# Adding transfers of a recurrence stage issued from one spaced list that is held during norms, with more descriptor space and later taps

## The chip, the cores and the metric

The kernel runs on one core of one Trainium2 chip. The metric is the device time of one launch in microseconds (us), the median of several executions. The core has five engines that run their own instruction streams: TensorE (PE) for matrix products, VectorE (DVE) and ScalarE (ACT) for elementwise work, GpSimd (POOL), and SyncE (SP), which here does nothing but issue transfers. Transfers move between the device memory (DRAM) and the on-chip memory by 16 DMA engines. They are issued on two queues: SP's, and POOL's own, which the profile calls software dynamic and whose descriptors are written into a small space on the chip; its size is an argument of the program (`dynamic_dma_scratch_size`). [...]

## The reference, cut to what matters

A decoder trunk of two layers on a sequence of 1024 vectors of 1024 numbers, all in float32. Layer 0 mixes by a gated recurrence with 8 heads, layer 1 by a causal convolution of width 31; behind each stands a layer norm, a squared-ReLU network of width 4096, and another layer norm.

```python
for i in range(DEPTH):
    mix = hgrn2_mixer(...) if i % 2 == 0 else conformer_conv_mixer(...)
    x = layer_norm(DEEPNORM_ALPHA * x + mix, ...)
    ff = jnp.square(jax.nn.relu(x @ ffn_w1[i])) @ ffn_w2[i]
    x = layer_norm(DEEPNORM_ALPHA * x + ff, ...)

def hgrn2_mixer(h, w_in, lb, norm_g, w_out):
    q, fz, v, g = jnp.split(h @ w_in, 4, axis=-1)
    f = lb + (1 - lb) * sigmoid(fz); k = 1 - f; q = silu(q)
    o = recurrence(q, k, v, cumsum(log f))      # S_t = diag(f_t) S_{t-1} + k_t v_t,  o_t = S_t q_t
    o = o * lax.rsqrt(jnp.mean(jnp.square(o), axis=-1, keepdims=True) + RMS_EPS)   # the norm of a head
    return (o * norm_g * silu(g)) @ w_out
```

## The kernel before, in words

Each float32 product is made of three products of a cheaper kind (high by high, high by low, low by high part). Larger products are moreover done on 2 by 2 blocks with 7 products for 8; their operands are sums of blocks, the "forms", which are numbered 1 to 7 and run in the order `ORDER` (1, 2, 6, 5, 7, 3, 4).

For the second matrix of each network (`ffn_w2`, 16 blocks of 4 parts in all, each part 0.5 MB) these sums of blocks are made in DRAM by transfers alone, with no engine's arithmetic. One such **chain** is written by `block_sums` (L401): two copies of 1 MB (L419 and L420), an accumulate of 1 MB onto what the first copy wrote (L421), and two accumulates of 0.5 MB, each onto the next slice (L423, twice). Each accumulate needs what the one before it wrote, so POOL, which issues all of them, waits for the landing of the last before it issues the next. Twelve chains are issued during the recurrence stage, one at every sixth form; the others come later, beside the network, and there `block_sums` is called with `after` or `adds`.

The **recurrence stage** takes the span from about 60 to 440 us. It interleaves two things. One is twelve pairs of half-width products (`PAIRS`: eight for q and forget gate, four for the output gate), 7 forms each, with weight blocks loaded as `pr` (L585), forms made from them as `fs`, and results copied out by `evacuate` (t at L837). The other is the recurrence of the eight heads, each a Python generator (`recurrence(h)`) that issues one small step whenever `slot()` calls `step()`. Time in the program is counted in **ticks**, one for each slot of three matrix products. `later(n, job)` has a job issued n ticks on. All engines are under a manual schedule here, so this order of writing is the order in which each engine runs; nothing is reordered afterwards. Outside this stage a scheduler sets the order.

At its end a head yields its two **norms**, one for each half of the sequence. `settle(half)` lets ScalarE square the outputs (L735), POOL scale the sum and raise it to the power -1/2 (L736, and L518 in `power_m_half`), and, 4 ticks later, ScalarE scale the outputs (L741); `give(half)` then lets TensorE transpose them (`ident,o`). The norms of a head come as a pair, a few us apart; there are 16. Outputs go to DRAM (`od`), come back (`u`, L962 and others), are multiplied by the gate, and stored again (`zd`, L924).

The **seam** (`seam()`) is the last stretch of the stage: within the last gate pair the output matrix `wout` is loaded (L940), the gated heads come back (L950), and the last head fetches its values at L632 (`f<-vd`, two loads of 256 KB) only just ahead of use, into a buffer that has just become free.

In the convolution stage (about 1125 to 1500 us) the 31 taps of each channel are scalars in a small table `par`, loaded at the start; ScalarE (L1591), VectorE (L1603) and POOL share the convolution. Products run beside it, in the order of `SEQ`, with weights that are either read from DRAM ready made (`wa<-ready`, L81) or loaded raw (L90) and split by ScalarE and VectorE (L72). There are three raw buffers, and a load into one first waits on POOL by a copy of one column (L86).

Of the kernel before, what the change touches and what calls it, by code (L numbers as in the profile page):

```python
# [8 lines left out]
F32 = mybir.dt.float32  # L9
# [3 lines left out]
ALU = mybir.AluOpType  # L13
PSUM = bass.MemoryType.PSUM

P = 128
# [15 lines left out]
QSCALE = 2.0**-30  # L32

NRM, LB, BPW1, BDW, CLG, CLB, TAP = 0, 8, 16, 32, 40, 48, 56
NPAR = TAP + KB * TAPS

KBYTES = 220
PAIRS = [("q", 0), ("q", 1), ("q", 2), ("q", 3), ("g", 0), ("q", 4), ("q", 5), ("q", 6), ("g", 1), ("q", 7), ("g", 2), ("g", 3)]
NPOOL = (12, 11)
SEQ = "P00 P01 P02 P03 P04 P05 P06 P07 P10 P11 P12 P13 N0 P14 F0 P15 S0 P16 P17 UA0 UA1 E2 E3 N1 E4 F1 E5 E6 S1 E7 UB0 UB1 L2 L3 L4 L5 L6 L7"  # L40
# [228 lines left out]
def body(ctx, tc, d, out):  # L269
# [100 lines left out]

    order = ExitStack()
    order.enter_context(tc.manual_schedule(engines={getattr(mybir.EngineType, e) for e in ("PE", "Pool", "SP", "DVE", "Activation")}))
    par = cst.tile([P, NPAR], F32, name="par")
    ident = cst.tile([P, P], F32, name="ident")
    wide_t, rows = (HT,), (NTB, P)

# [3 lines left out]
    vd = [[dram.tile([P, NTB, HT], F32, name=f"vd{m}{n}") for n in range(2)] for m in range(2)]  # L380

    ticks, waiting = [0], []

    def later(n, job):
        if n:
            waiting.append((ticks[0] + n, job))
        else:
            job()

    def tick(n=1):  # L390
        for _ in range(n):
            ticks[0] += 1
            for at, job in [w for w in waiting if w[0] <= ticks[0]]:
                waiting.remove((at, job))
                job()

    sums = {}

    def block_sums(name, layer, c, after=None, gap=0, adds=None):

        t = sums[name, layer, c] = dram.tile([4, P, 1024], F32, name=f"sum_{name}{layer}{c}")  # L401
        v, w = t.rearrange("a p n -> p a n"), d[name][layer, c].rearrange("a p n -> p a n")
        queue = nc.sync if after is not None else nc.gpsimd
        if adds is not None:

            def copies(rows, after):
                nc.sync.dma_start(out=t[0:4:2, rows.start, 0:1], in_=after)
                queue.dma_start(out=v[rows, 0:2], in_=w[rows, 0:4:2])
                queue.dma_start(out=v[rows, 2:4], in_=w[rows, 0:2])

            copies(slice(16, P), after)
            adds.append(lambda after: copies(slice(0, 16), after))
            adds.append(lambda after: nc.gpsimd.dma_start(out=v[:, 0:2], in_=w[:, 2:4], accum_op=ALU.add))
            for i in (2, 3):
                adds.append(lambda after, i=i: nc.gpsimd.dma_start(out=v[:, i], in_=v[:, i - 1], accum_op=ALU.add, max_dma_last_dim=4096))
            return
        if after is not None:
            nc.sync.dma_start(out=t[0:4:2, 0, 0:1], in_=after)
        queue.dma_start(out=v[:, 0:2], in_=w[:, 0:4:2])  # L419
        later(gap // 2, lambda: queue.dma_start(out=v[:, 2:4], in_=w[:, 0:2]))  # L420
        parts = [lambda: nc.gpsimd.dma_start(out=v[:, 0:2], in_=w[:, 2:4], accum_op=ALU.add)]  # L421
        for i in (2, 3):
            parts.append(lambda i=i: nc.gpsimd.dma_start(out=v[:, i], in_=v[:, i - 1], accum_op=ALU.add, max_dma_last_dim=4096))  # L423
# [83 lines left out]
    load_v(a2, 1, 0)  # L507
    load_v(a3, 1, 2)
    load_x(x11, 1, 4)
    nc.sync.dma_start(out=par, in_=d["par"])  # L510
    make_identity(nc, ident)
    nhalf = cst.tile([P, 8], F32, name="nhalf")
    nc.gpsimd.memset(nhalf, -0.5)
    qs = cst.tile([P, 1], F32, name="qs")
    nc.gpsimd.memset(qs, QSCALE)

    def power_m_half(dst, src, n):
# [116 lines left out]
    def recurrence(h):  # L634
# [96 lines left out]
        def settle(half):  # L731
            ss = stat.tile([P, 2, 4], F32, tag="ss", name="ss")
            cs = range(half * NTB, half * NTB + NTB)
            for c in cs:
                nc.scalar.activation(o[:, c], out_ps[:, c, :], AF.Square, scale=1.0 / QSCALE, accum_out=ss[:, 0, c % NTB : c % NTB + 1])  # L735
            nc.gpsimd.tensor_scalar(out=ss[:, 1], in0=ss[:, 0], scalar1=1.0 / P, scalar2=RMS_EPS, op0=ALU.mult, op1=ALU.add)  # L736
            power_m_half(ss[:, 0], ss[:, 1], 4)

            def rest():
                for c in cs:  # L740
                    nc.scalar.activation(o[:, c], out_ps[:, c, :], AF.Copy, scale=ss[:, 0, c % NTB : c % NTB + 1])  # L741
                later(1, lambda: ready.add(half))

            later(4, rest)
# [262 lines left out]
    for p, (kind, j) in enumerate(PAIRS):  # L1007
        st = {"banks": dict(turn_of)}
        turn_of = {"z": turn_of["a"], "a": turn_of["b"], "b": turn_of["z"]}
        pace[1] = 0.0 if p == 0 else 0.6 if p < 3 else 0.5  # L1010
        if kind == "g" and p < len(PAIRS) - 1:
            to_load += [(2 * j, 0), (2 * j + 1, 1), (2 * j, 1), (2 * j + 1, 0)]
        if p == len(PAIRS) - 1:
            seam()
        for i in ORDER:
            if kind == "q" and i == 2:
                while any(a[0] <= j - 3 for a in active) or recs and recs[0] <= j - 3:
                    tick()
# [15 lines left out]
    while step():  # L1034
        tick()
    tick(100)
    assert not waiting and not loaded and not to_load and not gates, (waiting, gates)
    order.close()
    oT = [o[0] for o in oT]

# [187 lines left out]
    class Up:  # L1228
# [14 lines left out]
        def settle(self, c):  # L1243

            for q in range(2):
                self.first(self.of[c], q)
# [291 lines left out]
    assert not ahead and not staged  # L1538


    nc.sync.dma_start(out=sm[:, :2], in_=d["lmix"])
    rings["mm"] = bank((1, 5, 2, 6))
    stA = {"hr": ring(run(0, 2, 8), (8, 256), "ha"), "r": ring(run(16, 2, 2), wide_t, "r")}
# [29 lines left out]
        bg.jobs.append(conv[-1])  # L1573

    def tap(j, i):
        return par[:, TAP + j * TAPS + i : TAP + j * TAPS + i + 1]

    def convolve_pool(half, j, u, sums):

# [380 lines left out]
```

## Time and profile before

| what | value |
| --- | --- |
| median of 3 runs | 2057.19 us (2056.47 to 2060.54) |
| profiled execution | 2057.16 us |
| its span, first to last instruction | 2055.4 us |
| recurrence stage, TensorE busy | 371.18 of 380.00 us (from 60 to 440) |
| convolution stage, TensorE busy | 373.08 of 375.00 us (from 1125 to 1500) |
| transfers on POOL's queue, whole span | 58.72 MB, 12.2% of the 16 DMA engines |

A row of the timeline gives the start in us, the time of the group in us, engine, line, operation, tiles (output<-inputs) and, in brackets, how long the engine had stood idle before and for what. "SPq" and "PEld" are SP's issues and TensorE's weight loads. In the view of waits, "issue" stands for time in which the engine waited for nothing that the profile shows. "DMA to landing" is the time from the issue of a transfer to the landing of its last byte.

### The profile page before, as it was taken

The page shows a single profiled execution, that of the slowest core. Times are in us where ns is not written, and L with a number is a line of the kernel's source. Part 1 is how long each engine was busy: PE and PEld are TensorE (multiplying, and loading weights), DVE is VectorE, ACT ScalarE, POOL GpSimd, SP SyncE. Part 2 cuts the span into 40 slices and gives each one's busy share as a digit, 9 for nine tenths or more (in the row PEclk, how much of TensorE's full clock was granted, in tenths as well). Part 3 has the DMA queues.
Part 4 walks back from the last instruction along what each step waited for, and adds up shares of the span by engine and source line. Part 5 has one row for each costly group of instructions (what it writes and reads, how often), then busy time and mean ns, then how long its engine had stood idle before and what let it go on. Part 6 is the DMA issues. An engine that isn't in the chain of part 4 may idle for free. (4 is left out here: it accounts for less than half of the span.)

```text
span 2055.4 us, 29649 instructions
## 1 busy us (share of the span) xinstructions
PE 2023.6 (98%) x11144; PEld 1669.0 (81%) x11144; DVE 1488.1 (72%) x1978; ACT 1094.5 (53%) x1725; POOL 396.3 (19%) x405
## 2 busy tenths in 40 slices
PE   8999999999999999999999999999999999999998
PEld 7888887888787888888888888888888878888886
DVE  8698888877856675665567897889589666754456
ACT  5456565631655556444443776498615555443343
POOL 0112232111101000000001798089110000100002
PEclk9999999999999999999999999999999999999999
DMA  4778999842679776989998744496759768995542
GB/s 187 221 201 229 265 254 269 248 183 85 192 268 295 281 282 225 394 329 329 338 335 299 298 185 184 180 351 247 276 216 337 231 225 303 391 292 195 195 154 103
DMA packets 183944, 517.55 MB, mean 252 GB/s; under 512 B 17912, under 2 KB 49784, under 8 KB 182776
## 3 DMA queue, kind: packets, MB, share of 16 engines
q1 hardware_dynamic: 168312, 456.93, 61.7%
q0 software_dynamic: 15488, 58.72, 12.2%
q8 instruction: 87, 1.43, 0.3%
q14 instruction: 57, 0.47, 0.1%
HBM read 380.85 MB, written 201.85 MB: 283 GB/s over the span
## 5 line engine op out<-in xcount | busy, mean ns | idle before, releaser
L204 PE MATMUL ps<-dw,dh 128*128 128x512 f32 x2688 | 611.3, 389 | 0.5 <-DVE dh L204 0.5
L204 PEld LDWEIGHTS ps<-dw,dh 128*128 128x128 f32 x2688 | 504.3, 188 | 105.3 <-DVE dh L204 0.9
L204 PE MATMUL ps<-x1f,fw 128*128 128x512 f32 x1344 | 307.5, 390 | 5.2 <-ACT c L1266 2.3
L204 PEld LDWEIGHTS ps<-x1f,fw 128*128 128x128 f32 x1344 | 251.5, 188 | 59.7 <-issue 2.5
L204 PE MATMUL ps<-xf,fs 128*128 128x512 f32 x1008 | 248.6, 397 | 3.6 <-issue 1.7
L204 POOL TENSOR_TENSOR cb<-cb,prod 128x512 f32<-128x512 f32 x168 | 223.2, 1337 | 13.0 <-ACT prod L1591 2.4
L204 PEld LDWEIGHTS ps<-xf,fs 128*128 128x128 f32 x1008 | 184.0, 188 | 42.6 <-issue 1.9
L204 DVE TENSOR_TENSOR dh<-dh 128x1024 fp32r<-128x1024 f32 x112 | 136.5, 1222 | 109.4 <-ACT dh L72 109.3
L204 DVE SCALAR_TENSOR_TENSOR ps<-u,par,ps 128x512 f32<-128x512 f32 x296 | 206.0, 750 | 10.6 <-ACT ps L1603 9.3
L204 PE MATMUL ps<-xa,wa 128*128 128x512 f32 x864 | 203.3, 392 | 0.2
L72 ACT CAST dh<-dh 128x1024 fp32r<-128x1024 f32 x112 | 117.5, 1051 | 143.9 <-DMA dh<-hf 137.7
L72 ACT CAST dw<-dr 128x1024 fp32r<-128x1024 f32 x112 | 117.4, 1054 | 140.9 <-PE ps L204 125.5
L204 DVE TENSOR_TENSOR dw<-dr,dw 128x1024 fp32r<-128x1024 f32 x112 | 136.3, 1223 | 76.6 <-ACT dw L72 75.8
L204 PEld LDWEIGHTS ps<-xa,wa 128*128 128x128 f32 x864 | 160.3, 188 | 33.6 <-DMA wa<-ready 0.6
L1591 ACT ACTIVATE prod<-u,par 128x512 f32<-128x512 f32 x168 | 119.4, 726 | 34.2 <-POOL cb L204 33.5
L518 POOL TENSOR_TENSOR mv<-mv,nhalf 128x1 f32<-128x1 f32 x32 | 42.2, 1321 | 405.1 <-DVE mv L204 394.8
L204 PE MATMUL ps<-w,oT 128*128 128x512 f32 x384 | 89.9, 392 | 1.3 <-ACT oT L932 0.8
L204 PE MATMUL ps<-xb,wa 128*128 128x512 f32 x384 | 91.1, 393 | 0.0
L204 PE MATMUL ps<-vw,xf 128*128 128x512 f32 x336 | 79.9, 400 | 5.6 <-ACT vw L435 5.3
L204 PEld LDWEIGHTS ps<-w,oT 128*128 128x128 f32 x384 | 71.4, 188 | 16.6 <-ACT oT L932 1.2
L204 PEld LDWEIGHTS ps<-xb,wa 128*128 128x128 f32 x384 | 71.1, 188 | 14.3
L204 PEld LDWEIGHTS ps<-vw,xf 128*128 128x128 f32 x336 | 65.0, 194 | 20.1 <-ACT vw L435 5.3
(250 smaller groups left out, 2891.9 us busy)
## 6 DMA issues: line engine op xcount, KB each, us to landing
wa<-ready SPq DMA_DIRECT2D x140, 512.0 KB, 5.0
dh<-hf SPq DMA_DIRECT2D x112, 512.0 KB, 5.3
sum_w<-in_w_dram POOLq DMA_DIRECT2D x40, 1024.0 KB, 10.0
ready<-spare SPq DMA_DIRECT2D x76, 512.0 KB, 5.7
raw<-in_w1q_dram SPq DMA_DIRECT2D x66, 512.0 KB, 4.3
dr<-sum_w SPq DMA_DIRECT2D x64, 512.0 KB, 5.5
hf<-ht SPq DMA_DIRECT2D x112, 256.0 KB, 4.9
dr<-in_w_dram SPq DMA_DIRECT2D x48, 512.0 KB, 5.3
```

The lines of the kernel that those rows point to most:

```text
L72: self.nc.scalar.copy(out=slot[:, 0, c], in_=raw[:, c])
L204: return op(*args, **kw)
L518: nc.gpsimd.tensor_tensor(out=dst, in0=src, in1=nhalf[:, :n], op=ALU.pow)
L1591: nc.scalar.activation(tp, u[:, k : k + HT], AF.Copy, scale=tap(j, k))
```

## The change: what it does

1. **One list.** A chain's transfers no longer come at fixed numbers of ticks after one another. Called with `turns=True`, `block_sums` puts the chain's four parts (both copies as one part, then the three accumulates) into the list `adding`. After every tick `add_some()` issues at most one part: of the oldest chain whose last part was issued at least `SPACE` = 16 ticks ago, and if the last part of any chain was issued at least 4 ticks ago.
2. **Held during norms.** While `quiet[0]` is above zero `add_some` issues nothing. It is raised when a head's last steps begin (before `outer`) and lowered when the second `settle` has been issued.
3. **Space.** `dynamic_dma_scratch_size` grows from 1024 to 2048 bytes. To make room, `par` is cut to its first 56 columns, and the 248 columns of taps become a tile of their own, `taps`, loaded by SP at the end of layer 0's network (L1560 of the changed kernel). Two small constants share a tile.
4. **Raw buffers.** The convolution's raw buffers go from three to two.

```diff
-    par = cst.tile([P, NPAR], F32, name="par")
+    par = cst.tile([P, TAP], F32, name="par")
...
+    adding, quiet, added = [], [0], [0]
...
                 waiting.remove((at, job))
                 job()
+            add_some()
+
+    def add_some():
+        for one in adding:
+            if not quiet[0] and one[0] <= ticks[0] and added[0] <= ticks[0]:
+                one.pop(1)()
+                one[0], added[0] = ticks[0] + SPACE, ticks[0] + SPACE // 4
+                if len(one) == 1:
+                    adding.remove(one)
+                break
...
-        queue.dma_start(out=v[:, 0:2], in_=w[:, 0:4:2])
-        later(gap // 2, lambda: queue.dma_start(out=v[:, 2:4], in_=w[:, 0:2]))
-        parts = [lambda: nc.gpsimd.dma_start(out=v[:, 0:2], in_=w[:, 2:4], accum_op=ALU.add)]
+
+        def copies():
+            queue.dma_start(out=v[:, 0:2], in_=w[:, 0:4:2])
+            queue.dma_start(out=v[:, 2:4], in_=w[:, 0:2])
+
+        parts = [copies, lambda: nc.gpsimd.dma_start(out=v[:, 0:2], in_=w[:, 2:4], accum_op=ALU.add)]
         for i in (2, 3):
             parts.append(lambda i=i: nc.gpsimd.dma_start(out=v[:, i], in_=v[:, i - 1], accum_op=ALU.add, max_dma_last_dim=4096))
-        for i, part in enumerate(parts):
-            later((i + 1) * gap, part)
+        if turns:
+            adding.append([ticks[0], *parts])
+        else:
+            for part in parts:
+                part()
...
+        quiet[0] += 1
         outer(range(NTB))
         later(1, lambda: chain(range(NTB)))
...
-        later(1, lambda: settle(1))
+        later(1, lambda: (settle(1), quiet.append(quiet.pop() - 1)))
...
-                block_sums(*to_sum.pop(0), gap=12)
+                block_sums(*to_sum.pop(0), turns=True)
...
-    wa = Slots(nc, vector, slots([192, 200, 208, 96, 104, 176], "wa"), raws(run(20, 3, 4)))
+    wa = Slots(nc, vector, slots([192, 200, 208, 96, 104, 176], "wa"), raws(run(20, 2, 4)))
...
+    taps = view(28, (KB * TAPS,), F32, "taps")
+    nc.sync.dma_start(out=taps, in_=d["par"][:, TAP:])
...
-    nc = _bacc.Bacc("TRN2", target_bir_lowering=False, num_devices=1, dynamic_dma_scratch_size=1024)
+    nc = _bacc.Bacc("TRN2", target_bir_lowering=False, num_devices=1, dynamic_dma_scratch_size=2048)
```

In the changed kernel the lines move: the copies stand at L432 and L433, the accumulates at L435 (1 MB) and L437 (0.5 MB), the norm's steps on POOL at L753 and L535. The order of TensorE within the recurrence is the same as before. What moves is POOL's.

The first place is POOL's stream around the two pairs of norms near 260 and 300 us of the span. Before (`sum_w` with a number is the tile of one chain, `ss` the sums of a norm):

```order
L423 DMA sum_w_2229<-sum_w_2229 128x1024
L419 DMA sum_w_2457<-in_w_dram 128x2x1024
L420 DMA sum_w_2457<-in_w_dram 128x2x1024
L736 TENSOR_SCALAR ss<-ss 128x4
L518 TENSOR_TENSOR ss<-ss,nhalf 128x4
L423 DMA sum_w_2229<-sum_w_2229 128x1024
L421 DMA sum_w_2457<-in_w_dram 128x2x1024
L736 TENSOR_SCALAR ss<-ss 128x4
L518 TENSOR_TENSOR ss<-ss,nhalf 128x4
L423 DMA sum_w_2457<-sum_w_2457 128x1024
```

And in the changed kernel, from the same norm on (the last two norm rows of the pair, then the group up to the next pair):

```order
L753 TENSOR_SCALAR ss<-ss 128x4
L535 TENSOR_TENSOR ss<-ss,consts 128x4
L437 DMA sum_w_1958<-sum_w_1958 128x1024
L437 DMA sum_w_2224<-sum_w_2224 128x1024
L432 DMA sum_w_2453<-in_w_dram 128x2x1024
L433 DMA sum_w_2453<-in_w_dram 128x2x1024
L432 DMA sum_w_2709<-in_w_dram 128x2x1024
L433 DMA sum_w_2709<-in_w_dram 128x2x1024
L437 DMA sum_w_2224<-sum_w_2224 128x1024
L435 DMA sum_w_2453<-in_w_dram 128x2x1024
L435 DMA sum_w_2709<-in_w_dram 128x2x1024
L753 TENSOR_SCALAR ss<-ss 128x4
```

The two transfers that stood between the norms of a pair are gone, and nine stand together behind it; those of one chain alternate with those of another.

The second place is POOL's stream from the last pair but one of norms to the last pair, at the seam. Before:

```order
L736 TENSOR_SCALAR ss<-ss 128x4
L518 TENSOR_TENSOR ss<-ss,nhalf 128x4
L736 TENSOR_SCALAR ss<-ss 128x4
L518 TENSOR_TENSOR ss<-ss,nhalf 128x4
L423 DMA sum_w_3502<-sum_w_3502 128x1024
L736 TENSOR_SCALAR ss<-ss 128x4
L518 TENSOR_TENSOR ss<-ss,nhalf 128x4
```

In the changed kernel:

```order
L753 TENSOR_SCALAR ss<-ss 128x4
L535 TENSOR_TENSOR ss<-ss,consts 128x4
L753 TENSOR_SCALAR ss<-ss 128x4
L535 TENSOR_TENSOR ss<-ss,consts 128x4
L437 DMA sum_w_3237<-sum_w_3237 128x1024
L437 DMA sum_w_3497<-sum_w_3497 128x1024
L437 DMA sum_w_3237<-sum_w_3237 128x1024
L437 DMA sum_w_3497<-sum_w_3497 128x1024
L753 TENSOR_SCALAR ss<-ss 128x4
L535 TENSOR_TENSOR ss<-ss,consts 128x4
```

Four accumulates of 0.5 MB, of the last two chains, stand where one stood.

The third place is POOL's stream in the convolution (`cb<-cb,prod` are its adds, `raw<-xa` the one-column copies that a raw load waits for). Before:

```order
L1586 COPY cb<-xa 128x1
L86 COPY raw<-xa 128x1 x3
L204 TENSOR_TENSOR cb<-cb,prod 128x512 x2
L518 TENSOR_TENSOR mv<-mv,nhalf 128x1
L204 TENSOR_TENSOR cb<-cb,prod 128x512 x68
```

In the changed kernel:

```order
L1606 COPY cb<-xa 128x1
L86 COPY raw<-xa 128x1 x2
L204 TENSOR_TENSOR cb<-cb,prod 128x512 x2
L535 TENSOR_TENSOR mv<-mv,consts 128x1
L204 TENSOR_TENSOR cb<-cb,prod 128x512 x53
L86 COPY raw<-xa 128x1
L204 TENSOR_TENSOR cb<-cb,prod 128x512 x15
```

The third copy, and with it the third raw load, moves from ahead of the adds to 15 adds before their end. On SP the load of the taps stands between two loads `wa<-ready`.

More of the change, by code (lines that the diff above doesn't have):

```diff
@@ L34 @@
 NRM, LB, BPW1, BDW, CLG, CLB, TAP = 0, 8, 16, 32, 40, 48, 56
-NPAR = TAP + KB * TAPS
 KBYTES = 220
+SPACE = 16
 PAIRS = [("q", 0), ("q", 1), ("q", 2), ("q", 3), ("g", 0), ("q", 4), ("q", 5), ("q", 6), ("g", 1), ("q", 7), ("g", 2), ("g", 3)]
@@ L395, in tick, with block_sums @@
                 job()
+            add_some()
[7 more added lines that the diff above has]
+                break
     sums = {}
-    def block_sums(name, layer, c, after=None, gap=0, adds=None):
+    def block_sums(name, layer, c, after=None, turns=False, adds=None):
         t = sums[name, layer, c] = dram.tile([4, P, 1024], F32, name=f"sum_{name}{layer}{c}")
@@ L509, in body @@
     load_x(x11, 1, 4)
-    nc.sync.dma_start(out=par, in_=d["par"])
+    nc.sync.dma_start(out=par, in_=d["par"][:, :TAP])
     make_identity(nc, ident)
-    nhalf = cst.tile([P, 8], F32, name="nhalf")
+    consts = cst.tile([P, 8], F32, name="consts")
+    nhalf, qs = consts[:, :7], consts[:, 7:]
     nc.gpsimd.memset(nhalf, -0.5)
-    qs = cst.tile([P, 1], F32, name="qs")
     nc.gpsimd.memset(qs, QSCALE)
@@ L1036, in body @@
     tick(100)
-    assert not waiting and not loaded and not to_load and not gates, (waiting, gates)
+    assert not waiting and not loaded and not to_load and not gates and not adding, (waiting, gates, adding)
     order.close()
@@ L1575, in tap @@
     def tap(j, i):
-        return par[:, TAP + j * TAPS + i : TAP + j * TAPS + i + 1]
+        return taps[:, j * TAPS + i : j * TAPS + i + 1]
     def convolve_pool(half, j, u, sums):
```

## The prediction

> **What bounds the kernel now.** I read the first part of the page, then the stage table, then the waits of TensorE (PE) and GpSimd (POOL) inside the recurrence, because the adding transfers stand only there. The profiled execution took 2057.16 us, of which the span is 2055.4; 1.76 us lie around it. It stands at the median of the runs (2057.19, from 2056.47 to 2060.54), so I forecast against it unchanged.
>
> ```profile
> span 2055.4 us, 29649 instructions
> PE 2023.6 (98%) x11144; PEld 1669.0 (81%) x11144; DVE 1488.1 (72%) x1978; ACT 1094.5 (53%) x1725; POOL 396.3 (19%) x405
> ...
> 60.00:440.00 380.00, 371.18 (x3744) 306.85 (x3743) 305.70 (x486) 223.81 (x507) 79.42 (x94) 1.00 0.88 248
> ```
>
> TensorE is busy 98%, at a granted clock of 1.00 in the stage row. That row (from 60 to 440 us, columns length, then busy time of PE, weight loads, DVE, ACT, POOL, then clock, DMA share, GB/s) leaves TensorE idle for 380.00 - 371.18 = 8.8 us. The product count doesn't change, so 8.8 us is the most that this stage could give back, and much of it has nothing to do with these transfers. The two largest of its waits, and the largest of POOL's, from 100 to 440 us (total us, times, longest):
>
> ```profile
> PE ps L204 <- issue: 1.7, 1, 1.7
> PE ps L204 <- DVE state L204: 1.4, 2, 0.9
> ```
> ```profile
> POOL sum_w L423 <- DMA sum_w<-in_w_dram: 89.3, 11, 11.6
> POOL ss L736 <- ACT o L735: 69.3, 15, 22.5
> POOL sum_w L421 <- issue: 35.3, 7, 7.9
> ```
>
> POOL stands still for most of the stage on its own transfers, yet 15 of its 16 norm steps (L736, then the power at L518) still wait for ScalarE's squares: POOL was there first. One norm of sixteen is late because of a transfer. That is the small target.
>
> **Part 1: no adding transfer ahead of a norm, and twice the descriptor space.** The one late norm:
>
> ```profile
> 252.00 1.02 POOL L420 DMA_DIRECT2D sum_w<-in_w_dram  x1
> ...
> 262.26 0.23 ACT L735 ACTIVATION_READ_ACCUMULATOR o<-ps 128x1 f32 x1
> 263.26 1.22 POOL L421 DMA_DIRECT2D sum_w<-in_w_dram  x1 [3.68 <-issue]
> 264.56 0.72 POOL L736 TENSOR_SCALAR ss<-ss 128x4 f32<-128x4 f32 x1
> 266.76 1.15 ACT L741 ACTIVATE o<-ps,ss 128x128 f32<-128x128 f32 x4 [1.94 <-POOL ss L518]
> 267.96 0.66 PE L204 MATMUL ps<-ident,o 128*128 128x128 f32 x4 [0.71 <-ACT o L741]
> ```
> ```profile
> DMA to landing us min/median/max: 10.9/10.9/10.9
> ```
>
> The squares end at 262.26 + 0.23 = 262.49. POOL is then stuck at the adding transfer L421. That transfer reads what the first copy wrote, but it starts 0.3 us after the second copy lands (252.00 + 10.9 = 262.9), under the label "issue": it is room for descriptors that it waits for, which is how I read all seven such waits. The norm begins at 264.56, some 2 us late, and TensorE loses 0.71 us; so about 1.3 us of lateness is free. In the changed order nothing stands between the two norms, and this stall goes: **-0.7 us** (bounds -0.7 and 0, if another wait follows at once). With 2048 bytes L421 could follow the first copy, but its later start held nothing else up: 0.
>
> A second stall belongs to the transfers by what is in flight:
>
> ```profile
> 329.96 0.88 POOL L423 DMA_DIRECT2D sum_w<-sum_w  x1 [3.55 <-DMA sum_w<-sum_w]
> ...
> 331.56 0.44 SPq L924 DMA_DIRECT2D zd<-t  x1
> ...
> 342.37 0.59 ACT L837 COPY t<-ps 128x512 f32<-128x512 f32 x1 [1.72 <-DMA zd<-t]
> ...
> 343.00 2.09 PE L204 MATMUL ps<-xf,fs 128*128 128x512 f32 x8 [0.31 <-ACT t L837]
> ...
> 346.81 1.09 PE L204 MATMUL ps<-xf,fs 128*128 128x512 f32 x4 [1.71 <-issue]
> ```
>
> A store of 256 KB (zd) issued at 331.56 isn't done at 342.3, 10.8 us later, with an accumulate of 0.5 MB and two copies of 1 MB beside it. ScalarE can't refill its buffer, and TensorE loses 0.31 and then 1.71 us. The pairs of norms on POOL around here:
>
> ```profile
> 299.77 0.19 POOL L736 TENSOR_SCALAR ss<-ss 128x4 f32<-128x4 f32 x1 [0.27 <-ACT o L735]
> ...
> 304.96 0.73 POOL L736 TENSOR_SCALAR ss<-ss 128x4 f32<-128x4 f32 x1 [2.83 <-ACT o L735]
> ...
> 345.64 0.19 POOL L736 TENSOR_SCALAR ss<-ss 128x4 f32<-128x4 f32 x1 [3.07 <-ACT o L735]
> ...
> 375.39 0.19 POOL L736 TENSOR_SCALAR ss<-ss 128x4 f32<-128x4 f32 x1 [0.57 <-ACT o L735]
> ```
>
> In the changed order the group behind 305 has four accumulates of 0.5 MB, two copies and one accumulate of 1 MB each, 5 MB; at 5 us a MB (the second copy above took 10.9 us, in which both copies moved 2 MB) it is over at about 331. I count **-2.0 us**, bounds -2.0 and 0.
>
> **Part 2: what has been held comes in bursts.** The same bytes now move in the windows behind the pairs of norms. Three places could pay. (a) Late loads of weight blocks: `pr` loads, made 5 to 10 us ahead of TensorE, already took up to
>
> ```profile
> DMA to landing us min/median/max: 14.1/14.1/14.1
> ```
>
> (the load issued between 225 and 245 us) without a gap on TensorE. I take 0, bounds 0 and +4 (two more stalls like the 2.0 us above). (b) A burst that isn't issued in full when the next pair of norms comes: behind 264.56 two accumulates of 0.5 MB and four copies, 5 MB and 25 us, have to land before the last two accumulates can be issued, by 293, where the next norm comes at 299.77; behind 345.64 it is 4.5 MB, by 370, and the norm comes at 375.39. I take 0; at 8 us a MB the second would land near 383 and hold the norm 7 us, of which 1.3 are free: about +6. (c) The **seam** at the end: in the order, four accumulates of 0.5 MB stand behind the last pair but one of norms, where one stood.
>
> ```profile
> 375.00:380.00 5.00, 5.00 (x32) 4.43 (x31) 4.89 (x8) 1.84 (x7) 1.22 (x2) 1.00 0.66 105
> 380.00:385.00 5.00, 5.00 (x148) 4.17 (x147) 4.89 (x10) 4.50 (x19) 2.04 (x3) 1.00 0.14 13
> 385.00:390.00 5.00, 5.00 (x41) 3.86 (x43) 4.96 (x11) 3.12 (x6) 0.00 (x0) 1.00 0.95 234
> 390.00:395.00 5.00, 4.64 (x114) 3.36 (x109) 4.77 (x8) 1.84 (x5) 0.00 (x0) 1.00 0.97 348
> 395.00:400.00 5.00, 5.00 (x54) 4.27 (x51) 3.25 (x5) 4.87 (x8) 0.00 (x0) 1.00 1.01 345
> ```
> ```profile
> 382.99 0.89 POOL L423 DMA_DIRECT2D sum_w<-sum_w  x1
> ...
> 391.68 0.56 SPq L632 DMA_DIRECT2D f<-vd  x1
> ...
> 400.94 1.16 PE L204 MATMUL ps<-f,kt 128*128 128x128 f32 x8
> ...
> 405.29 0.91 PE L204 MATMUL ps<-f,kt 128*128 128x128 f32 x6 [0.25 <-DMA f<-vd]
> ```
> ```profile
> DMA to landing us min/median/max: 8.7/8.7/8.7
> ```
>
> The first row holds one accumulate and nothing else (105 GB/s in 5 us is its 0.5 MB): 0.66 x 5 = 3.3 us of all DMA engines. Three more are 9.9 us. From 385 to 400 the engines are full (0.95, 0.97, 1.01). The last head's values (`f<-vd`) are issued at 391.68, land 8.7 us later at 400.4, and TensorE uses them at 400.94: 0.6 us to spare; for the second half it already waits 0.25 us. So the price runs from 0 to 9.9 - 0.6 = +9.3. Two accumulates start near 383, where the row from 380 to 385 shows idle engines, which covers some 2 us; the other two start when those land, about 390. If from there both queues get equal turns, the 8.7 us of work up to the landing gain 4 to 5 us, and the second half about one more: **+5.0 us**, near the middle. SP's own order hardly moves there.
>
> [...]
>
> **Part 3: taps and raw buffers in the convolution.**
>
> ```profile
> 1125.51 2.27 SPq L81 DMA_DIRECT2D wa<-ready  x4
> ...
> 1144.49 0.72 ACT L1591 ACTIVATE cb<-u,par 128x512 f32<-128x512 f32 x1
> ```
> ```profile
> 1399.07 45.47 POOL L204 TENSOR_TENSOR cb<-cb,prod 128x512 f32<-128x512 f32 x31 [0.47 <-ACT prod L1591]
> ...
> 1428.38 1.04 ACT L72 CAST wa<-raw 128x1024 fp32r<-128x1024 f32 x1
> ```
>
> The taps, 127 KB, are issued on SP near 1125.5, among loads that SP makes there anyway, and first used at 1144.49: 19 us of cover, 0. With two raw buffers for three, the load for step E6 waits for a small POOL copy that now stands 15 adds before the end of this run of 31 (1.47 us each): 1399.07 + 16 x 1.47 = 1422.5. These loads, from 1380 to 1450 us, took
>
> ```profile
> raw<-in_w1q_dram SPq DMA_DIRECT2D x3, 512.0 KB, 4.4
> ```
>
> 4.4 us (the last number), so it lands near 1427 before the split at 1428.38, with 1.4 us to spare. I take 0, bounds -1 (the earlier loads wait less for order) and +2 (should the adds run late).
>
> **Sum.** -0.7 - 2.0 + 0 + 0 + 5.0 + 0 = +2.3, so 2057.2 + 2.3 = **2059.5 us**.
>
> **Rivals.** (1) *The seam decides, slower*: the accumulates take their full turn ahead of the last head's values: +9.3 - 2.7 = +6.6, **2063.8**. For it: 0.6 us of slack and full engines; against: half of the added work starts in an idle stretch. From a price at the seam of 4.1 + 2.7 = 6.8 us on it makes the kernel slower by what can be measured. (2) *The bursts pay in the middle too*: +4 on (a) or +6 on (b) over my sum, about **2064**; for it the zd stall, against it the 14.1 us load that cost nothing. (3) *The seam is covered*: only the gains, -2.7, **2054.5**; for it the idle row at 380, against it the three full rows behind. (4) *All of the stage's waits were of this kind and go*, -8, **2049**: against it, 1.4 us wait for VectorE's state alone, which no transfer holds. (5) *It doesn't do what it says*: the waits of POOL move, and since 15 of 16 norms were never held, nothing on TensorE changes: **2057.2**.
>
> **How the numbers follow.** Forecast 0.36, (1) 0.15, (2) 0.12, (3) 0.16, (4) 0.06, (5) 0.15. A measurement of this kernel can tell about 0.2%, 4.1 us, from no change: below 2053.1 counts as faster, above 2061.3 as slower. Faster is (4) and the better half of (3): 0.15. Slower is (1), (2) and the tail of the forecast: 0.31. The rest, 0.54. The range from 2053 to 2065 leaves out (4) and the ends of (1) and (2); the forecast's own runs from 2056 to 2062.
>
> **What would show it.** Right: no ScalarE wait for `ss` and none for a `zd` store in the stage, rows "<- issue" gone from POOL's waits, and TensorE waits for `f<-vd` of several us near 400. Wrong: if `f<-vd` still lands in 9 us the seam term falls; if TensorE waits for `fs` or `pr` behind a burst, or a norm waits for an adding transfer, part 2's zeros fall; a wait for `wa` near 1428 refutes part 3.

## The result, and the profile after

The changed kernel takes 2078.09 us (median of 5 runs, 2076.52 to 2080.13), the kernel before 2059.04 us (5 runs beside them, 2056.47 to 2060.94): a ratio of 1.0091, 95% interval 1.0076 to 1.0107. It is slower by 19 us. The forecast was 2059.5, with a range up to 2065.

The changed kernel's page, its stage row, and then one short stretch of both kernels, from 100 to 120 us (before first, after second; columns as in the stage row: length, busy time of PE, weight loads, DVE, ACT, POOL, granted clock, DMA share, GB/s):

```profile
span 2074.7 us, 29652 instructions
...
60.00:440.00 380.00, 351.26 (x3638) 290.63 (x3637) 287.70 (x464) 212.76 (x495) 76.62 (x94) 0.97 0.84 233
```
```profile
100.00:120.00 20.00, 20.00 (x90) 16.54 (x89) 17.09 (x24) 11.45 (x18) 4.39 (x5) 1.00 0.92 233
```
```profile
100.00:120.00 20.00, 7.27 (x33) 5.68 (x31) 2.62 (x5) 2.42 (x4) 4.51 (x6) 0.76 1.05 269
```

The 19 us are lost inside the recurrence, and most of them in one place: in 20 us TensorE works 7.27 us where it worked 20, at a mean clock of 0.76, while the DMA engines are full (a share of 1.05). TensorE's order in this stage is the same in both kernels, so each product of one trace can be set beside the same product of the other. By how many us it comes later:

| place (us in the trace of before) | 106 | 135 | 260 | 300 | 340 | 390 | 415 | 440 | 1125 | end |
| --- | --- | --- | --- | --- | --- | --- | --- | --- | --- | --- |
| later by, us | 0.0 | 16.4 | 17.2 | 16.3 | 16.6 | 14.3 | 23.3 | 23.4 | 21.3 | 19.4 |

Two steps up, 16.4 near 110 and 9.0 at the seam, and two steps down, 0.9 at 268 and 2.3 between 340 and 390. TensorE's two largest waits name the steps up, and ScalarE's row (which makes the forms `fs`) says what the first one hangs on. (From 440 us to the end 4.0 us come back; two other traces, of experiments 4 and 6, lose 3.0 and 1.6 us there, so this part differs from trace to trace.)

```profile
PE ps L204 <- DVE t L204: 15.2, 3, 13.5
PE ps L204 <- DMA f<-vd: 6.8, 1, 6.8
```
```profile
ACT fs L631 <- DMA pr<-in_wp_dram: 21.2, 2, 16.3
```

**The first stall.** The changed kernel's timeline:

```profile
80.15 1.19 POOL L435 DMA_DIRECT2D sum_w<-in_w_dram  x1 [4.97 <-DMA sum_w<-in_w_dram]
80.86 1.18 POOL L432 DMA_DIRECT2D sum_w<-in_w_dram  x1
81.54 1.17 POOL L433 DMA_DIRECT2D sum_w<-in_w_dram  x1
...
87.14 2.04 SPq L649 DMA_DIRECT2D v<-vd  x2
...
89.22 36.22 SPq L602 DMA_DIRECT2D pr<-in_wp_dram  x6
...
113.86 0.62 ACT L631 CAST fs<-pr 128x512 fp32r<-128x512 f32 x1 [16.33 <-DMA pr<-in_wp_dram]
...
120.80 7.44 PE L204 MATMUL ps<-xf,fs 128*128 128x512 f32 x25 [13.53 <-DVE t L204]
```

POOL issues the first chain's 1 MB accumulate and, in the same breath, both copies of the second chain: 3 MB in flight at 82 us. Before, the second chain's copies came at 93.96, after the accumulate had landed. The weight load that SP issues at 89.2 lands, before and after, in

```profile
DMA to landing us min/median/max: 6.8/6.8/6.8
```
```profile
DMA to landing us min/median/max: 24.6/24.6/24.6
```

What the two queues moved from 80 to 120 us (packets, MB, share of the 16 engines' time; before first, after second; q0 is POOL's queue, q1 SP's):

```profile
q0 software_dynamic: 1618, 6.17, 65.7%
q1 hardware_dynamic: 3071, 3.98, 32.6%
```
```profile
q0 software_dynamic: 2180, 8.32, 79.9%
q1 hardware_dynamic: 2488, 2.92, 25.5%
```

POOL's queue moves 2.15 MB more in the same time, and SP's 1.06 MB less. The 1.06 MB are four weight loads of 256 KB that SP hasn't issued yet: in this stretch the kernel before issues eight, which land in 2.4 to 6.8 us, and the changed kernel four, which land in 23.5 to 24.6; its fifth comes at 123.9 us, after the stall. TensorE stands waiting for forms made of those late four.

**The seam.** Four accumulates of 0.5 MB of two chains, the last three each held until the accumulate before it in its own chain has landed (for the second of them that is one of 1 MB), and the last head's values between them:

```profile
397.35 0.92 POOL L437 DMA_DIRECT2D sum_w<-sum_w  x1
400.37 0.84 POOL L437 DMA_DIRECT2D sum_w<-sum_w  x1 [2.10 <-DMA sum_w<-in_w_dram]
404.18 0.81 POOL L437 DMA_DIRECT2D sum_w<-sum_w  x1 [2.97 <-DMA sum_w<-sum_w]
405.96 0.69 SPq L649 DMA_DIRECT2D f<-vd  x1
410.49 0.80 POOL L437 DMA_DIRECT2D sum_w<-sum_w  x1 [5.50 <-DMA sum_w<-sum_w]
...
422.21 2.05 PE L204 MATMUL ps<-f,kt 128*128 128x128 f32 x8 [6.83 <-DMA f<-vd]
```
```profile
DMA to landing us min/median/max: 16.1/16.1/16.1
```

The first load of `f<-vd` lands after 16.1 us (8.7 before), and TensorE waits 6.8 us.

### The profile page after: what moved, and what is told of

It is laid out like the page before. It is cut to its first block, busy times and chain, and to the rows that moved or that the text cites. A ratio compares the mean times of both kernels' runs of the same rounds, so it can differ in the third digit from the quotient of the medians.

```text
span 2074.7 us, 29652 instructions
## 1 busy us (share of the span) xinstructions
PE 2025.1 (98%) x11144; PEld 1672.6 (81%) x11144; DVE 1487.2 (72%) x1978; ACT 1092.8 (53%) x1725; POOL 398.2 (19%) x405
## 5 line engine op out<-in xcount | busy, mean ns | idle before, releaser
L204 PE MATMUL ps<-xf,fs 128*128 128x512 f32 x1008 | 251.4, 401 | 16.1 <-DVE t L204 15.2
L204 DVE SCALAR_TENSOR_TENSOR ps<-u,taps,ps 128x512 f32<-128x512 f32 x296 | 206.2, 750 | 12.1 <-ACT ps L1623 10.8
L1611 ACT ACTIVATE prod<-u,taps 128x512 f32<-128x512 f32 x168 | 119.9, 726 | 40.4 <-POOL cb L204 39.8
L535 POOL TENSOR_TENSOR mv<-mv,consts 128x1 f32<-128x1 f32 x32 | 42.5, 1329 | 406.9 <-DVE mv L204 396.6
L204 PEld LDWEIGHTS ps<-w,oT 128*128 128x128 f32 x384 | 71.4, 188 | 16.6 <-ACT oT L950 1.2
L204 PEld LDWEIGHTS ps<-xb,wa 128*128 128x128 f32 x384 | 71.1, 188 | 14.4
L204 DVE TENSOR_TENSOR fs<-pr,fs 128x512 fp32r<-128x512 f32 x72 | 49.2, 684 | 45.7 <-ACT fs L631 45.7
```

Of the source, the lines that this page charges most:

```text
L204: return op(*args, **kw)
L535: nc.gpsimd.tensor_tensor(out=dst, in0=src, in1=nhalf[:, :n], op=ALU.pow)
L1611: nc.scalar.activation(tp, u[:, k : k + HT], AF.Copy, scale=tap(j, k))
```

## The experiments

All times are medians beside runs of the kernel before on the same chip (2059.6 to 2061.0 us in the four sets of runs); the ratio is to those.

**1. Space or order?** Two of the change's parts could put 3 MB in flight: 2048 bytes of descriptor space, and the list's order. First, the changed order with the old space:

```diff
-    nc = _bacc.Bacc("TRN2", target_bir_lowering=False, num_devices=1, dynamic_dma_scratch_size=2048)
+    nc = _bacc.Bacc("TRN2", target_bir_lowering=False, num_devices=1, dynamic_dma_scratch_size=1024)
```

> The changed kernel with 1024 bytes of descriptor space in place of 2048; nothing else differs, so POOL's order is the changed one. Theory S (the doubled space let the second chain's copies, at 80.9 us, and the first chain's 1 MB accumulate stand in flight together, 3 MB, ahead of the weight loads): the copies are held, TensorE's wait near 107 to 121 us (13.5 us) shrinks to under 2 us, and the time is about 2078 - 15 = 2063 us. Theory O (the list's order does it, whatever the space: the copies of the second chain no longer stand behind the first chain's 0.5 MB accumulate): the wait stays above 10 us, about 2077 us. In between (one of the two copies still gets ahead): a wait of 4 to 8 us, 2066 to 2071 us. Both expect the wait for f<-vd at the seam unchanged at about 7 us.

Measured: 2062.58 us, ratio 1.0018 (1.0006 to 1.0029). Its waits of TensorE and POOL:

```profile
PE ps L204 <- DMA f<-vd: 6.0, 1, 6.0
PE ps L204 <- DVE t L204: 2.1, 2, 1.8
```
```profile
POOL sum_w L435 <- issue: 69.1, 10, 8.2
```

The first stall is gone but for 1.8 us; the seam's is not. What holds the burst back is the wait for room: POOL stands 69.1 us ahead of the 1 MB accumulates alone, under the label "issue", which none of its waits has in the changed kernel. Theory S, as worded for this run, holds in wait and time. In order it is the case in between: the first copy of the second chain still starts at 84.74 us, 4 us behind the accumulate, and the second waits until 94.32. With these 2 MB ahead of them the weights landed in 9.1 to 10.4 us.

Then the old order with the new space, everything else as changed:

```diff
         if turns:
-            adding.append([ticks[0], *parts])
+            queue.dma_start(out=v[:, 0:2], in_=w[:, 0:4:2])
+            later(6, lambda: queue.dma_start(out=v[:, 2:4], in_=w[:, 0:2]))
+            for i, part in enumerate(parts[1:]):
+                later((i + 1) * 12, part)
```

> The changed kernel, space of 2048, taps and raw buffers included, but with the adding transfers issued at fixed numbers of ticks as in the kernel before (gap 12, second copy after 6). Theory O: both large stalls are the order's, so the wait near 110 us is gone and f<-vd is back at 0.3 us; about 2058 us, no difference from the kernel before that can be told. Theory S: deeper queues by themselves lengthen the weight loads, so some of the 13.5 us stays, 2062 us or more. What differs from the kernel before in the convolution is the price of taps and raw buffers alone: 0, at most 1.3 us.

Measured: 2054.23 us, ratio 0.997 (0.996 to 0.9981): faster, which neither theory had. So neither half alone makes the big stall. The space without the list is a gain; the list without the space costs 0.2%, with the seam's 6 us in it; both together cost 0.9%. In the old order the second chain's copies stand behind the first chain's first accumulate of 0.5 MB, which has to wait for a landing (12.06 us in this trace, the copies at 94.46 and 95.17 us), and so they can't run ahead, with 1024 bytes or with 2048.

The order with both, changed only at the start, so that the second and third chain's copies come behind that accumulate again:

```diff
         for one in adding:
+            if len(one) == 5 and len(sums) <= 3 and one is not adding[0] and len(adding[0]) > 2:
+                continue
             if not quiet[0] and one[0] <= ticks[0] and added[0] <= ticks[0]:
```

> The changed kernel with one rule more at the start: the second and third chain's copies aren't issued until the chain ahead has issued its first 0.5 MB accumulate, as it was in the kernel before; space 2048 and all else as changed, and the chains after it run up to one group later. Theory O with sharing (the weight load at 89.2 us landed after 24.6 us in place of 6.8 us because 2 MB more were in flight): the wait near 110 us is gone and 16 us come back, about 2062 us, the seam's 7 to 8 us staying. Rival (the first gap has another cause, a late store or the norms' hold): the wait stays, about 2078 us. Rival 2 (wherever two chains' copies stand together the weight loads run late, so the gap only moves to the next group): a new wait of 5 us or more on weights between 157 and 215 us, 2067 us or more.

Measured: 2075.32 us, ratio 1.0071 (1.0044 to 1.0099). The wait near 110 us is gone, and another of the same size has come 107 us later:

```profile
221.47 0.69 DVE L204 TENSOR_TENSOR total<-pr 128x512 f32<-128x512 f32 x1 [5.58 <-DMA pr<-in_wp_dram]
222.25 0.62 ACT L633 CAST fs<-total 128x512 fp32r<-128x512 f32 x1 [14.69 <-DVE total L204]
226.70 0.97 ACT L743 COPY kt<-ps 128x512 f32<-128x512 f32 x2
227.34 1.01 PE L204 MATMUL ps<-v,kt 128*128 128x128 f32 x3 [13.81 <-ACT kt L743]
```

TensorE's row names ScalarE's `kt`, but ahead of `kt` in ScalarE's stream stands a form, where it has waited 14.69 us for a sum that VectorE made only when the weights had landed. So it is the weights again: the load issued at 191.5 us takes 23.7 us, and VectorE waits for the next until 221.47. The chains held at the start had moved into the group behind the pair of norms at 186 to 190 us, where two accumulates of 0.5 MB, one of 1 MB and two copies now start between 191 and 198 us. This is rival 2, larger than it expected and at the end of its window (the wait lasts from 213.5 to 227.3 us): the gap isn't bound to its place, it follows the burst.

**2. One number: 12 for 16.**

```diff
-SPACE = 16
+SPACE = 12
```

> One number changed: SPACE from 16 to 12, so a chain's parts stand 12 ticks apart and those of two chains 3; 2048 bytes, the hold as changed. Then the second chain's copies stand behind the first chain's first 0.5 MB accumulate, and two accumulates stand at the seam where the change has four. Theory (how many MB stand in flight at once decides, and the order sets that): no wait over 2 us near 110 us, a wait for f<-vd of 2 to 4 us, 2060 to 2063 us. Rival (any spaced list with the hold bunches and stalls somewhere, as the run with the second chain held did near 220 us): a wait of 5 us or more somewhere between 110 and 390 us, 2068 us or more.

Measured: 2058.9 us, ratio 0.9999 (0.9988 to 1.0011), a little less than the theory's 2060 to 2063. The same kernel again:

> SPACE of 12 for 16 again, to have its trace beside the others of this call: its time was that of the kernel before (2058.9 us beside 2059.6). Theory: no wait of over 2 us near 110 us, and for f<-vd 1 to 4 us with two accumulates at the seam; the norms are in time; what keeps it from the 2054 us of the old order with 2048 bytes must be the seam or single late weight loads. Rival: a stall of 3 us or more remains somewhere else in the recurrence.

Measured: 2056.72 us, ratio 0.9977 (0.9968 to 0.9987); the two measurements of the kernel differ by 0.2%. Its trace (its own time, 2059.42 us, is the longest of ten) has no stall near 110 us. What is left stands at the seam, with two accumulates, and in one wait of 3.0 us that ends at 221 us; 14 of 16 norms are in time, where all were expected:

```profile
PE ps L204 <- DMA f<-vd: 4.0, 2, 2.1
PE ps L204 <- DVE state L204: 3.5, 2, 3.0
```

Four ticks in one constant are worth 20 us. Near 110 us they put the second chain's copies (94.50 us) behind the first chain's 0.5 MB accumulate, which waits for a landing. List, hold and space stay as changed here; none of them has to cost anything.

The size of a burst alone doesn't decide, though. In this same trace a 1 MB accumulate and two copies start together at 104 to 106 us, and the weight loads issued at 112.0 and 115.8 us land in 8.7 and 7.2 us. In the changed kernel's own trace 4.5 MB are issued between 207 and 210 us and 5 MB between 281 and 285, and up to the seam no wait of TensorE is over 1.7 us. What makes the bursts at 80 and 191 us worse, no run isolates. Both have two loads of values (`v<-vd`) issued just ahead of the weights; experiment 6 moves those.

**3. The hold.** The changed kernel without it:

```diff
-        quiet[0] += 1
         outer(range(NTB))
...
-        later(1, lambda: (settle(1), quiet.append(quiet.pop() - 1)))
+        later(1, lambda: settle(1))
```

> The changed kernel without the hold during norms: the list, SPACE of 16 and 2048 bytes stay. POOL's order up to the first norm is the same, so by the theory (the list's order puts two chains' copies together at the start, where no norm is near) the wait of 13 to 14 us near 110 us stays; at the seam three accumulates stand behind the first norm of the last pair but one, so f<-vd still waits 4 to 7 us; some norms are late again by 1 to 2 us: about 2076 us. Rival (the hold makes the bursts): both waits fall under 3 us, about 2062 us.

Measured: 2078.41 us, ratio 1.0087 (1.0062 to 1.0112). The time and the first wait are about what the theory expected; the seam's wait is shorter, in a trace whose own time, 2068.97 us, is the shortest of four, and no norm is late: POOL is in time for all 16. So the hold isn't what makes the first burst. Nor is it needed for the norms once there are 2048 bytes; with the hold and 1024 bytes (the first run of experiment 1) 14 of 16 are in time.

```profile
PE ps L204 <- DVE t L204: 12.8, 3, 12.1
PE ps L204 <- DMA f<-vd: 2.5, 1, 2.5
```

**4. The seam.** One more hold, from the seam's start to the last head's second norm; one accumulate stays where one was before, three come behind the last norms:

```diff
         if p == len(PAIRS) - 1:
             seam()
+            quiet[0] += 1
...
-        later(1, lambda: (settle(1), quiet.append(quiet.pop() - 1)))
+        later(1, lambda: (settle(1), quiet.append(quiet.pop() - 1 - (h == H - 1))))
```

> The changed kernel with one more hold: from the start of the seam to the last head's second norm no adding transfer is issued, so one accumulate of 0.5 MB stands behind the last pair but one of norms, as before, and three come after the last pair. Seam theory (the three further accumulates delay f<-vd from 8.7 to 16.1 us to landing, 6.8 us on TensorE and about 1.5 more while its clock recovers): the wait for f<-vd falls under 1 us and the time to about 2078 - 8 = 2070 us. Rival (f<-vd is late because the stretch before it moved, and the wout loads are what it queues behind): the wait stays at 5 us or more, 2077 us. The wait near 110 us stays at 13 to 14 us by either.

Measured: 2071.35 us, ratio 1.0056 (1.0038 to 1.0073), 7 us less than the changed kernel. TensorE no longer waits for `f<-vd`, whose two loads both take 9.1 us to landing:

```profile
DMA to landing us min/median/max: 9.1/9.1/9.1
```

The stretch before had moved here too, by 14 us at 260 us and 11 at 390, so it isn't that. The three accumulates are the cause of the seam's wait.

Both single repairs together (1024 bytes and the seam's hold):

> The two single repairs together: the changed kernel with 1024 bytes of descriptor space and with the hold from the seam's start to the last head's second norm. Theory (two separate causes, the deep burst near 110 us and the accumulates at the seam, whose prices add): neither TensorE's wait near 110 us nor the one for f<-vd of 6 us, so 2062.6 - 7 = about 2055.5 us, 4 to 5 us faster than the kernel before. Rival (the three accumulates that come after the last norms collide with the loads that follow the seam): the 6 us come back between 430 and 560 us, 2061 us.

Measured: 2058.14 us, ratio 0.9987 (0.9976 to 0.9999): both stalls are gone, and the ratio is 0.3% below that of 1024 bytes alone, about the 7 us expected of the seam. The gain over the kernel before is 0.1% where 0.2% was expected: the prices add, roughly.

**5. Taps and raw buffers, and what the space is worth.** The old order with 1024 bytes, so that only part 3 of the change is left:

```diff
-    nc = _bacc.Bacc("TRN2", target_bir_lowering=False, num_devices=1, dynamic_dma_scratch_size=2048)
+    nc = _bacc.Bacc("TRN2", target_bir_lowering=False, num_devices=1, dynamic_dma_scratch_size=1024)
```

(against the kernel with the old order and 2048 bytes)

> The kernel before in everything that concerns the adding transfers (fixed ticks, 1024 bytes), but with the taps loaded later and two raw buffers: part 3 of the change alone. Prediction's step (part 3 costs and gains nothing, -1 to +2): 2060 us beside the kernel before at 2060, and then the 6 us that the old order with 2048 bytes gained are the space's. Rival (the convolution's part gained them): about 2055 us. In the trace of the old order with 2048 bytes the convolution and what follows is 1.5 to 3 us shorter than before and the recurrence 0.5 to 1 us, so I expect 2057 to 2058.

Measured: 2059.95 us, ratio 1.0000 (0.9989 to 1.0012). Part 3 costs and gains nothing; the 2057 to 2058 us that were read from one trace didn't come. So what the old order with 2048 bytes gained is the space's. The same kernel a second time:

> The kernel with the old order (fixed ticks) and 2048 bytes, taps and raw buffers as changed, timed again beside the next one, because its gain of 6 us was not expected. Theory (the space alone puts all 16 norms in time, where 5 of 16 were late in the trace of the same order with 1024 bytes; 3 to 5 us on TensorE): again 4 to 6 us faster than the kernel before, a ratio of 0.997 to 0.998. Rival (the gain was the draw of the runs): a ratio of 0.999 to 1.000.

Measured: 2052.58 us, ratio 0.9956 (0.9944 to 0.9969). POOL's waits in the norms, with 1024 bytes first, with 2048 bytes second:

```profile
POOL ss L756 <- ACT o L755: 58.5, 11, 21.2
POOL sum_w L435 <- issue: 41.2, 7, 6.8
```
```profile
POOL ss L756 <- ACT o L755: 91.2, 16, 23.3
```

With 1024 bytes POOL was in time for 11 of 16 norms, with 2048 for all 16, and the row "<- issue" is gone. TensorE waits 3.7 us for the scaled outputs `o` in the first trace, and 0.4 us in the second. One of the late ones, and the same norm in the other kernel:

```profile
267.16 1.22 POOL L435 DMA_DIRECT2D sum_w<-in_w_dram  x1 [5.92 <-issue]
268.46 0.19 POOL L756 TENSOR_SCALAR ss<-ss 128x4 f32<-128x4 f32 x1
...
270.99 0.66 PE L204 MATMUL ps<-ident,o 128*128 128x128 f32 x4 [2.09 <-ACT o L761]
```
```profile
259.46 1.55 POOL L435 DMA_DIRECT2D sum_w<-in_w_dram  x1
262.76 0.19 POOL L756 TENSOR_SCALAR ss<-ss 128x4 f32<-128x4 f32 x1 [1.75 <-ACT o L755]
...
267.24 0.60 PE L204 MATMUL ps<-ident,o 128*128 128x128 f32 x4
```

With room, the accumulate is issued 7.7 us earlier and out of the norm's way. Product by product, the trace with 2048 bytes is 4.6 us ahead at the end of the recurrence, and 4.7 at the end of the span. The times differ by 6 to 8 us, so a part of the gain isn't in this pair of traces.

On top of that, the last chain's last accumulate was moved behind the seam:

```diff
-                later((i + 1) * 12, part)
+                later((i + 1) * 12 + (60 if i == 2 and len(to_sum) == 4 else 0), part)
```

> The same with one part moved: the last accumulate of the last chain, which stands behind the last pair but one of norms and beside the loads of the seam, comes 60 ticks later, behind the last pair. Seam theory (every accumulate beside the last head's values costs up to 3 us): the waits for f<-vd, 1.2 us with the old order, fall to 0.3 or less, and the time by about 1 us, to some 2053 us where the other stands at 2054. Rival (one accumulate is covered by the idle stretch at 380 to 385 us): no difference.

Measured: 2052.0 us, ratio 0.9958 (0.9945 to 0.9971), not to be told from the 2052.58 beside it, though `f<-vd` is no longer among TensorE's waits. These two are the fastest kernels of the study: the old order, 2048 bytes, and the later taps that make room for them.

**6. Does it matter what stands ahead of the weights on SP's queue?** The changed kernel, with the first two loads of values behind the four weight loads:

```diff
-    for i in range(2):
-        load_values(i)
+    later(22, lambda: [load_values(i) for i in range(2)])
```

> The changed kernel (list, SPACE 16, hold, 2048 bytes) with one thing moved on SP's queue: the first head's two loads of values, v<-vd, 256 KB each in rows of 512 bytes, issued at 87 us just ahead of the four weight loads that TensorE then waits for, come 22 ticks later, behind those four. POOL's transfers are untouched. Theory of shares (while 3 MB stand in flight on POOL's queue, SP's queue gets only a third of the DMA engines' time or less, and the two value loads, which landed 16.6 and 23.7 us after their issue, use it up ahead of the weights): the weights land about 8 us earlier, TensorE's wait near 110 us falls from 13.5 to 3 to 6 us, and the time to about 2068 us. Rival (what SP issues waits until the 3 MB ahead on POOL's queue have landed, whatever stands between): the wait stays at 11 us or more, about 2077 us.

Measured: 2077.81 us, ratio 1.0073 (1.0048 to 1.0097): no gain, and yet neither side was right. The weights do land earlier, in 12.8 us where it was 24.6, and the wait of 13.5 us near 110 us is gone:

```profile
DMA to landing us min/median/max: 12.8/12.8/12.8
```
```profile
PE ps L204 <- DVE blocks L204: 2.8, 1, 2.8
PE ps L204 <- DVE T L204: 2.1, 1, 2.1
PE ps L204 <- DVE t L204: 1.8, 1, 1.8
```

But at 135 us (as placed in the trace of before) TensorE is 10.8 us late all the same, in smaller gaps up to 137 us and with its clock at half from 136 to 143, and by 260 us 14.4. What is late now are the next weight loads, issued from 110.7 us on:

```profile
129.04 0.62 ACT L631 CAST fs<-pr 128x512 fp32r<-128x512 f32 x1 [9.07 <-DMA pr<-in_wp_dram]
```

From 130 to 136 us the DMA engines are idle (shares of 0.03, 0.00 and 0.00 in 2 us each), and VectorE, busy 1.97, 1.97 and 2.00 us of 2, works off what had to wait. So the delay is passed on, from one set of loads to the next and then to VectorE. That something on SP's queue has to wait out the whole burst is refuted only just: the first weight load lands at 100.5 us, 1.3 us ahead of the last of the 3 MB (101.8). The expected gain is refuted by the time.

## Why the prediction was wrong, point by point

- **Part 1, the late norm, -0.7, and the `zd` stall, -2.0: right.** The two steps down in the table are 0.9 and 2.3 us, and all 16 norms find POOL waiting (165.9 us, 16 times, in the trace of after). The reason given, that nothing stands between the norms of a pair, isn't the only one: the late norm is in time without the hold, and in the old order too once there are 2048 bytes. The step of the `zd` stall is the list's: the wait stays in the old order with either space (1.9 and 1.6 us near 345 us) and is gone under the list with 1024 bytes. But both steps were read as all that the norms were worth, from one execution with one late norm. The other trace of that order and space has five.
- **"With 2048 bytes L421 could follow the first copy, but its later start held nothing else up: 0": wrong.** The space alone is worth 6 to 8 us, the largest gain in the change. The row that said so was quoted, 35.3 us of POOL's waiting for "issue", and read rightly as a wait for room (under the old order 41.2 us of it with 1024 bytes, and no such row with 2048); it was priced only where it had met a norm in that trace.
- **Part 2 (a), late weight loads, 0 with bounds 0 and +4: the step that failed.** It measured +16.4. The bound was made from stalls behind norms in the middle of the stage, and from a load of 14.1 us that cost nothing there. The burst that decided stands at the stage's start, where there is no norm and no hold, and where the prediction didn't look at the order. In its place the runs show a weight load that takes 24.6 us where it took 6.8, behind an accumulate and two copies issued in one breath, and a wait of 13.5 us that is gone with 1024 bytes, with the old order, or with 12 ticks for 16. Which property of that burst makes the loads so late stays open. The rival on bursts had the mechanism, with 4 to 6 us as its price.
- **Part 2 (b), bursts that hold up a norm, 0: right.** None did in the changed kernel.
- **Part 2 (c), the seam, +5.0 with bounds 0 and +9.3: right in mechanism, and at the upper end in size.** The load took 16.1 us where 8.7 plus 4 to 5 was expected, TensorE waited 6.8 us, and the step is 9.0 with what follows. The 2 us of cover from the idle stretch at 380 us weren't there: only one of the four starts at the place of 383 us, the next two come 3 and 7 us later, and three of them ran beside the wout loads. `f<-vd` lands at 422.1 us, 3 us behind the last of the four, as at the upper bound. That both queues get equal turns was the author's assumption for the +5.0, and no run shows it: from 406 to 422 us POOL's queue had 43.6% of the DMA engines' time and SP's 59.8%, and the load took 16.1 us.
- **Missing from every price: the clock.** A stall was counted at its own length. The clock rows below show about 1.6 us more behind the first (3.2 us of work at half speed); the other 1.3 us of its 16.4 are a second wait for `t`, which ends at 137.45 us. Behind the seam's wait the clock is at 0.50 from 418 to 426 us and at 0.57 in the 2 us after, and 2.2 us more are lost.
- **Part 3, taps and raw buffers, 0: right.** Alone they give a ratio of 1.0000.
- **The chances.** Slower had 0.31, by the seam or the bursts. Both came, and the second at about four times its price of +4.

## What to carry to other kernels

A queue's small space can be a throttle that something else relies on, and a wait that looks like a waste may be what keeps a burst from running ahead: before enlarging it, list what the issuing engine could then issue without a wait, from the first transfer on, and not only around the place to be mended. Here the same doubling gained 0.3 to 0.4% under an order in which each chain's copies stand behind a transfer that must wait, and lost 0.7% under one in which they don't (from a ratio of 1.0018 to 1.0091). And a wait that differs from one execution to the next, like a late norm, is to be priced from more than one trace.

## What was not expected of the hardware

**The clock fell in the long stall, and stayed low after it.** The changed kernel from 106 us on (columns as above, the granted clock third from the right):

```profile
106.00:108.00 2.00, 1.27 (x6) 0.73 (x4) 0.00 (x0) 0.00 (x0) 0.21 (x1) 1.00 1.08 234
...
112.00:114.00 2.00, 0.00 (x0) 0.00 (x0) 0.00 (x0) 0.14 (x1) 0.26 (x1) 0.50 1.02 390
...
122.00:124.00 2.00, 2.00 (x6) 1.51 (x6) 1.27 (x3) 2.00 (x4) 0.00 (x0) 0.51 1.05 207
124.00:126.00 2.00, 2.00 (x10) 1.63 (x9) 1.30 (x3) 1.56 (x3) 0.00 (x0) 1.00 1.02 218
```

TensorE stops at about 107.3, its clock is at half by 112, and half it stays for some 3 us after work begins again at 120.80: 6 products in 2 us, then 10. The kernel before has no wait of TensorE over 1.7 us in this stage, and its stage row has 1.00. The clock fell after shorter waits too: in the run of experiment 6 the clock is at 0.53 from 136 to 138 us, after waits of 2.13 and 2.79 us with work between them (TensorE busy 0.38, 0.55 and 0.66 us in the three rows of 2 us from 132 us on).

**In the burst POOL's queue got most of the DMA engines' time, though not most of the packets.** From 87 to 104 us, with loads outstanding on both queues, the changed kernel's two queues had (packets, MB, share)

```profile
q0 software_dynamic: 889, 3.38, 73.6%
q1 hardware_dynamic: 1809, 1.72, 31.5%
```

Equal turns in time, as the seam was priced with, would have been half each. SP's queue moved twice as many packets and got less than half of the other's time; its packets are smaller (1.72 MB in 1809, against 3.38 MB in 889). Later its share falls further, to 13.7% from 100 to 120 us and 4.3% from 108 to 120, where it moves only 0.17 MB. So the four weight loads had moved most of their bytes by 108 us, and the rest took until 118.8. What sets the shares, the size of the packets or how many transfers stand in flight on each queue, and why so small a rest takes so long, no run tells apart.
